# Encoder trunk on one core: four steps of early output products ahead of the conv norm's sums on TensorE in place of two, four between sums and spread, eight behind

## The chip, the cores and the metric

The kernel runs on one core of a Trainium2 chip. A core has TensorE (matrix products), VectorE, ScalarE, GpSimd and SyncE, each with its own in-order list of instructions, which wait for one another through semaphores. TensorE reads its operands from SBUF and writes to PSUM, which has eight banks of 128 x 512 float32 values here. The metric is the device time of one execution in microseconds; the figure for a kernel is the median of its runs.

## The reference

Two layers are computed over a sequence of 512 tokens with 1024 features in float32. Each layer is

```python
x = x + 0.5 * swiglu(rms_norm(x, ffn1_norm[l]), ffn1_w_gate[l], ffn1_w_up[l], ffn1_w_down[l])
h = rms_norm(x, mix_norm[l])
p = h @ w_in[l]
attn = mla_group(...)      # latent attention, 8 heads of 64 value columns, chunk-causal
conv = conv_group(...)     # GLU, causal depthwise convolution (31 taps), layer norm, silu
x = x + jnp.concatenate([attn, conv], axis=-1) @ w_out[l]
x = x + 0.5 * swiglu(rms_norm(x, ffn2_norm[l]), ffn2_w_gate[l], ffn2_w_up[l], ffn2_w_down[l])
x = rms_norm(x, post_norm[l])
```

The part that matters here is the end of the mixing stage. The conv group closes with a layer norm over its 512 columns and a silu:

```python
mu = jnp.mean(xf, axis=-1, keepdims=True)
xc = xf - mu
y = xc * lax.rsqrt(jnp.mean(xc * xc, axis=-1, keepdims=True) + EPS)
return (y * g.astype(jnp.float32) + b.astype(jnp.float32)).astype(x.dtype)
```

Then the output projection takes 1024 columns, the first 512 from the attention heads and the last 512 from the conv group. Its sum over columns can begin with the attention half while the conv half is still being normed.

## The kernel before, in words

Activations lie transposed: 128 features on the partitions, 512 tokens along the row, so a 512-column group is four tiles of 128 x 512. A weight block is one 128 x 1024 tile that holds, for 128 output features, the eight 128 x 128 pieces over the 1024 input features.

Every large product is made of three in a rounded float32 form (`mm3`, L169): both operands are split into a high part and the remainder, and high x high (L170), high weight x low activation (L171) and low weight x high activation (L172) are summed in PSUM. The high part of a weight is a cast on ScalarE (L151). The low part of the first four blocks of the output projection is made by a copy of the negated weight and a DMA that adds (L154, L155), and that of the last four by a subtraction on GpSimd (L157).

The mixing stage of a layer is the function `mix_body`. The heads' work ends with pairs of heads: value products on TensorE (L917, in plain float32, half of the array's columns each), their scaling on VectorE (L920, which reads PSUM), and the split into high and low (L177 on ScalarE, L178 on VectorE). The four pairs give the attention half of the output projection's operand, the list `at`.

The conv group's norm runs beside the last heads, and is a chain over all engines:

- The sum over the four tiles goes through TensorE once (L999) to give the mean on all partitions. VectorE subtracts it from the four tiles (L1001).
- ScalarE squares each tile (L200 for the first, L203 for the other three) and VectorE adds the squares (L207, three additions).
- TensorE sums the squares over the partitions: the *sums* (L214, four small products).
- VectorE scales and adds epsilon (L221), GpSimd takes the power -1/2 (L189), VectorE lays the result on a diagonal (L229), and TensorE copies it to all partitions: the *spread* (L233).
- VectorE multiplies the four tiles by it (L1016), ScalarE applies gain, bias and silu (L1018), and the split follows (L177, L178). This is the conv half, the list `cv`.

The output projection has eight blocks of 128 output features. The first four get their attention half early, as filler between the pieces of that chain. These are the *early steps*: first three steps for each of the four blocks (one for each of the first three pairs of heads, which are complete), then one for each block with the last pair. That makes 16 steps, each of three products (L170 to L172):

```python
steps = [(m, k) for m in range(WOG) for k in range(3)] + [(m, 3) for m in range(WOG)]
...
early_steps(0, EA, heads[H - 1][EARLY])
...
early_steps(EA, EB, sums)
early_steps(EB, len(steps), spreading)
```

Each call carries a lower limit: its products come after the instruction named last (`issue_after`). The first call follows the last head's scores, the second the sums, the third the spread. The norm's chain between the calls is written with high priority. Within these limits a planner sets the order of every engine's list by simulating the program's timeline as it builds it. Then the conv half of blocks 0 to 3 follows, the addition to `x` (L1031), and blocks 4 to 7 in full. In the listings and profiles below the blocks' PSUM tiles are called `ps`, the norm's `cv`, weights' high and low parts `wh` and `wl`.

Of the kernel before, what the change touches and what calls it, by code (L numbers as in the profile page):

```python
# [50 lines left out]
GLUP = 0  # L51
EARLY = "s"
PRELOAD = 1
EA = 2
EB = 6
WOG = 4
CHAIN = 400
WAKE = 10
# [20 lines left out]
def encoder_kernel(ctx: ExitStack, tc: tile.TileContext, xT, consts, vecs, rgain, wgu1, wd1, wdq1,  # L79
# [33 lines left out]
    def tiny(tag, w, dt=FP):  # L113
        return small.tile([P, w], dt, tag=tag, name=nm(tag))
# [28 lines left out]
    def vv(l, name):  # L143
        o, w = VOFF[name]
        return vec[:, l, o:o + w]
# [487 lines left out]
    def mix_body(kpool, l, gx, norm, done):  # L633
# [350 lines left out]
        def early_steps(a, b, behind_):  # L984
            with tc.issue_after(behind_):
                for m, k in steps[a:b]:
                    if k == 0:
                        early.append(bank())
                    group(early[m], wo[m], at, (k,), KD)

        early_steps(0, EA, heads[H - 1][EARLY])
        st = Stats()
# [14 lines left out]
        if PRELOAD:  # L1007
            with behind(heads[H - 1]["exps"]):
                A.activation(tiny("pre", 1), ysum[:, 0:1], AF.Silu)
        early_steps(EA, EB, sums)  # L1010
        early_steps(EB, len(steps), spreading)
        lg, lb = vv(l, "lg"), vv(l, "lb")
# [283 lines left out]
```

## Time and profile before

| | us |
|---|---|
| median of three runs | 1797.07 |
| lowest and highest of them | 1794.69, 1797.32 |
| the profiled execution's own time | 1794.2 |
| its span, first to last instruction | 1792.4 |
| TensorE busy in the span | 1778.5 |
| VectorE, ScalarE, GpSimd busy | 1493.5, 1093.8, 382.1 |

TensorE's granted clock is full for the whole span. A busy TensorE means that products are in flight, not that they run at the peak rate. The stage of interest stands twice in the span, at about 495 to 530 us in the first layer and at about 1383 to 1418 us in the second. In a row of a timeline stand the start, the duration, the engine, the line, the operation, the tiles written and read, the shape, and in brackets the idle time of the engine before it with what ended it.

### The profile page before, as it was taken

Reading aid. Unit: us, or ns where it says so; the run is one execution under the profiler, and the core shown is the slowest. Engines: PE = TensorE matmul, PEld = TensorE weight load, DVE = VectorE, ACT = ScalarE, POOL = GpSimd, SP = SyncE. Lnnn points to the kernel's source line nnn. Section 1 sums busy time; section 2 is a strip of 40 time slices with the busy share of each in tenths; the row PEclk is TensorE's granted clock in tenths of the full one; section 3 lists DMA queues with packets and bytes.
Section 4 is the critical chain, followed back from the end, with each engine's and each line's share of the span. In section 5 each row is a group of like instructions: output and inputs, shape, how many; then the busy total and the mean of one; then the engine's idle time right before and its main releaser. Section 6 shows DMA issues by size and latency. Waiting matters only on the chain.

```text
span 1792.4 us, 29441 instructions
## 1 busy us (share of the span) xinstructions
PE 1778.5 (99%) x11430; PEld 1579.1 (88%) x11430; DVE 1493.5 (83%) x2309; ACT 1093.8 (61%) x1699; POOL 382.1 (21%) x313
## 2 busy tenths in 40 slices
PE   9999999999999999999999999999999999999998
PEld 7899999888678899999888999998976788999997
DVE  7898988689965989898779989876999568989883
ACT  5565756467853575756645757564778435756564
POOL 1000000248722000000310000002585310000002
PEclk9999999999999999999999999999999999999999
DMA  5657575324213466665426575743260126575742
GB/s 170 171 131 182 136 178 123 109 84 127 68 28 96 124 166 162 153 160 131 124 65 171 123 194 122 193 114 111 81 157 21 52 79 170 130 185 131 183 117 74
DMA packets 71947, 228.28 MB, mean 127 GB/s; under 512 B 8448, under 2 KB 9600, under 8 KB 71808
## 3 DMA queue, kind: packets, MB, share of 16 engines
q1 hardware_dynamic: 55536, 171.87, 30.5%
q0 software_dynamic: 16128, 54.53, 18.2%
q8 instruction: 89, 1.46, 0.3%
q14 instruction: 50, 0.41, 0.1%
q10 hardware_dynamic: 144, 0.00, 0.0%
HBM read 222.19 MB, written 2.10 MB: 125 GB/s over the span
## 4 chain that ended last, share of the span: by engine, by line
PE 90%; DVE 6%; ACT 1%; issue 1%; DMA 1%; POOL 0%; SPq 0%; ACTq 0%; DVEq 0%
PE ps L170 24%; PE ps L171 23%; PE ps L172 23%; PE ps L389 11%; PE ps L390 6%; DVE cv L968 1%; DVE mx L876 1%; DMA raw<-in_wgu 1%; PE ps L917 1%; DVE r L898 0%; PE ps L895 0%; PE ps L214 0%; DVE r L855 0%; PE ps L676 0%; DVE wl L262 0%
## 5 line engine op out<-in xcount | busy, mean ns | idle before, releaser
L171 PE MATMUL ps<-r,wh 128*128 128x256 f32 (+1 forms) x2556 | 812.9, 319 | 0.1
L170 PE MATMUL ps<-r,wh 128*128 128x256 f32 (+1 forms) x2556 | 811.0, 320 | 1.1 <-ACT wh L151 0.5
L172 PE MATMUL ps<-r,wl 128*128 128x256 f32 (+1 forms) x2364 | 755.3, 321 | 0.0
L170 PEld LDWEIGHTS ps<-r,wh 128*128 128x128 f32 x2556 | 483.8, 189 | 45.6 <-ACT wh L151 3.7
L171 PEld LDWEIGHTS ps<-r,wh 128*128 128x128 f32 x2556 | 484.6, 190 | 36.4 <-DVE r L178 1.5
L172 PEld LDWEIGHTS ps<-r,wl 128*128 128x128 f32 x2364 | 448.2, 190 | 33.8
L389 PE MATMUL ps<-xj,wh 128*128 128x512 f32 x864 | 303.8, 391 | 0.0
L151 ACT CAST wh<-raw 128x1024 fp32r<-128x1024 f32 (+3 forms) x148 | 132.6, 901 | 216.9 <-PE ps L171 135.3
L260 ACT CAST wh<-fr 128x1024 fp32r<-128x1024 f32 (+1 forms) x160 | 157.8, 986 | 103.8 <-DVE fr L426 49.3
L406 POOL DMA_DIRECT2D ls<-in_wgu x72 | 62.5, 868 | 734.5 <-ACT ls L405 525.0
L157 DVE TENSOR_TENSOR wl<-raw,wh 128x1024 fp32r<-128x1024 f32 (+3 forms) x132 | 141.2, 1077 | 91.0 <-ACT wh L151 90.3
L262 DVE TENSOR_TENSOR wl<-fr,wh 128x1024 fp32r<-128x1024 f32 (+1 forms) x160 | 181.8, 1136 | 20.1 <-ACT wh L260 20.1
L389 PEld LDWEIGHTS ps<-xj,wh 128*128 128x128 f32 x864 | 161.4, 188 | 30.1
L390 PE MATMUL ps<-xj,ls 128*128 128x256 f32 x576 | 161.3, 280 | 0.0
L974 POOL TENSOR_TENSOR y<-y,pr 128x495 f32<-128x495 f32 (+29 forms) x90 | 121.7, 1353 | 46.4 <-ACT pr L972 41.0
L260 ACT CAST wh<-raw 128x1024 fp32r<-128x1024 f32 (+1 forms) x100 | 98.1, 981 | 45.2 <-PE ps L171 24.5
L262 DVE TENSOR_TENSOR wl<-raw,wh 128x1024 fp32r<-128x1024 f32 (+1 forms) x100 | 113.3, 1133 | 14.2 <-ACT wh L260 13.8
L390 PEld LDWEIGHTS ps<-xj,ls 128*128 128x128 f32 x576 | 108.3, 188 | 0.0
L405 ACT ACTIVATE ls<-fr 128x1024 fp32r<-128x1024 f32 (+1 forms) x56 | 56.1, 1002 | 75.9 <-PE ps L390 42.8
L207 POOL TENSOR_TENSOR r<-r,t 128x512 f32<-128x512 f32 x45 | 73.3, 1638 | 136.5 <-ACT t L203 136.2
L968 DVE SCALAR_TENSOR_TENSOR cv<-m,vec,cv 128x511 f32<-128x511 f32 (+14 forms) x120 | 87.8, 732 | 3.8 <-ACT cv L964 2.2
L406 POOL DMA_DIRECT2D ls<-in_wdq x32 | 27.6, 863 | 262.1 <-ACT ls L405 262.1
(257 smaller groups left out, 2919.1 us busy)
## 6 DMA issues: line engine op xcount, KB each, us to landing
fr<-in_wgu SPq DMA_DIRECT2D x112, 512.0 KB, 4.3
ls<-in_wgu POOLq DMA_DIRECT2D x72, 512.0 KB, 6.3
raw<-in_wgu SPq DMA_DIRECT2D x62, 512.0 KB, 4.6
fr<-in_wdq SPq DMA_DIRECT2D x48, 384.0 KB, 5.0
ls<-in_wdq POOLq DMA_DIRECT2D x32, 384.0 KB, 4.8
raw<-in_wd SPq DMA_DIRECT2D x32, 384.0 KB, 3.2
raw<-in_wd SPq DMA_DIRECT2D x32, 256.0 KB, 2.8
raw<-in_wcv SPq DMA_DIRECT2D x16, 512.0 KB, 3.6
```

Of the source, the lines that this page charges most:

```text
L151: order["cast"] = A.copy(hi[:, :w], raw[:, :w]).ins
L157: (G if kind in POOLW.split() else V).tensor_tensor(lo[:, :w], raw[:, :w], hi[:, :w].bitcast(FP), ALU.subtract)
L170: T.matmul(o, lh, rh, start=first, stop=False, skip_group_check=free)
L171: T.matmul(o, lh, rl, start=False, stop=False, skip_group_check=free)
L172: order["mm"] = T.matmul(o, ll, rh, start=False, stop=last, skip_group_check=free).ins
L260: A.copy(hi[:, :w], src[:, :w])
L262: order["lo"] = V.tensor_tensor(lo[:, :w], src[:, :w], hi[:, :w].bitcast(FP), ALU.subtract).ins
L389: T.matmul(o, w[0][:, c], both, start=start and k == 0, stop=False, skip_group_check=True)
L390: last = T.matmul(o[:, 0:HS], w[1][:, c], both[:, 0:HS], start=False, stop=k == 3, skip_group_check=True).ins
L406: G.dma_start(out=lo[:, :n], in_=w, accum_op=ALU.add)
L968: V.scalar_tensor_tensor(acc[:, s:], u[c][:, :S - s], tap(k), acc[:, s:], ALU.mult, ALU.add)
L974: order["conv"] = G.tensor_tensor(ys[c][:, s:], ys[c][:, s:], pr[:, s:], ALU.add).ins
```

## The change

Two constants are different: the first call of early steps makes four steps in place of two, the second still makes four (the fifth to the eighth in place of the third to the sixth), and the third makes the last eight in place of the last ten. No instruction is added or left out.

```diff
-EA = 2
-EB = 6
+EA = 4
+EB = 8
```

The planner makes of it what follows; both layers change in the same way. On TensorE around the sums, `ps_5619` is block 0, `ps_5659` (before) and `ps_5629` (now) is block 1, `ps_5374` the last pair of heads. Ahead of the seven value products that complete this pair, the difference is

```order
 L171 MATMUL ps_5619<-r_5292,wh_5391 128x512
 L172 MATMUL ps_5619<-r_5291,wl_5393 128x512
+L170 MATMUL ps_5629<-m_5156,wh_5398 128x512
 L917 MATMUL ps_5374<-r_5339,m_4774 64x512
 L917 MATMUL ps_5374<-r_5303,m_4783 64x384
```

One product of block 1 went ahead of the seven. Behind them, on the same engine, there stood before

```order
L917 MATMUL ps_5374<-r_5303,m_4801 64x128
L917 MATMUL ps_5374<-r_5346,m_4801 64x128
L214 MATMUL cv_5643<-ones,m_4633 128x1 x4
L170 MATMUL ps_5619<-r_5357,wh_5391 128x512
L171 MATMUL ps_5619<-r_5358,wh_5391 128x512
L172 MATMUL ps_5619<-r_5357,wl_5393 128x512
L170 MATMUL ps_5659<-m_5156,wh_5398 128x512
```

and now there stands

```order
L917 MATMUL ps_5374<-r_5346,m_4801 64x128
L170 MATMUL ps_5619<-r_5357,wh_5391 128x512
L171 MATMUL ps_5619<-r_5358,wh_5391 128x512
L172 MATMUL ps_5619<-r_5357,wl_5393 128x512
L171 MATMUL ps_5629<-m_5157,wh_5398 128x512
L172 MATMUL ps_5629<-m_5156,wl_5400 128x512
L214 MATMUL cv_5650<-ones,m_4633 128x1 x4
L170 MATMUL ps_5629<-r_5291,wh_5398 128x512
```

The sums followed the last value product directly; now five products of blocks 0 and 1 stand between the two.

On VectorE at the same place, where `m_4633` collects the squares and `t_5383` takes the last pair of heads, the difference is

```order
 L207 TENSOR_TENSOR m_4633<-m_4633,m_4058 128x512
 L207 TENSOR_TENSOR m_4633<-m_4633,m_3846 128x512
+L207 TENSOR_TENSOR m_4633<-m_4633,m_4058 128x512
 L920 TENSOR_TENSOR t_5383<-ps_5374,t_5372 128x512
-L207 TENSOR_TENSOR m_4633<-m_4633,m_4058 128x512
 L178 TENSOR_TENSOR r_5386<-t_5383,r_5385 128x512
```

The last addition of squares moved ahead of the scaling of the last pair of heads.

On TensorE around the spread, where `ps_5669` is block 2, there now stands

```order
L172 MATMUL ps_5669<-r_5291,wl_5407 128x512
L233 MATMUL cv_5659<-m_4058,ones 128x512
L170 MATMUL ps_5669<-r_5357,wh_5405 128x512
L171 MATMUL ps_5669<-r_5358,wh_5405 128x512
L172 MATMUL ps_5669<-r_5357,wl_5407 128x512
```

Before, the spread (then `cv_5652`) stood six products earlier, ahead of all products of block 2; it still follows twelve products after the sums. Behind it stand 24 products in place of 30 until the first one that reads the conv half. In the conv half of blocks 0 to 3 the products are interleaved differently, so that block 0 ends six rows later. The lists of SyncE and GpSimd are the same.

## The prediction

> **What bounds the kernel now.** I read the page first, for the engine that fills the span and for the chain that ended last; then the waits of TensorE alone; then the timeline of TensorE, VectorE and ScalarE around the places where it waits.
>
> ```profile
> span 1792.4 us, 29441 instructions
> PE 1778.5 (99%) x11430; PEld 1579.1 (88%) x11430; DVE 1493.5 (83%) x2309; ACT 1093.8 (61%) x1699; POOL 382.1 (21%) x313
> PE 90%; DVE 6%; ACT 1%; issue 1%; DMA 1%; POOL 0%; SPq 0%; ACTq 0%; DVEq 0%
> ```
>
> TensorE is busy for 99% of the span and carries 90% of the last-ended chain. A change pays only if it closes a gap in TensorE's own stream, and a wait of another engine costs nothing until TensorE stands behind it. Its waits, by what ended them, are few:
>
> ```profile
> PE cv L214 <- DVE m L207: 2.8, 2, 1.4
> PE ps L853 <- DVE kn L822: 1.1, 2, 0.9
> PE ps L131 <- DVE ones L127: 1.1, 1, 1.1
> PE ps L872 <- ACT r L880: 0.5, 1, 0.5
> PE ps L170 <- ACT wh L151: 0.5, 2, 0.3
> PE ps L917 <- ACT r L880: 0.4, 2, 0.2
> PE ps L214 <- DVE r L207: 0.2, 1, 0.2
> ```
>
> The first row is the largest and sits exactly where the change works: the sums of the conv group's norm (L214) wait twice, once in each layer, 1.4 us each, for VectorE's last addition of squares (L207). No row names a DMA. The timeline of TensorE in the first layer:
>
> ```profile
> 503.13 0.39 PE L171 MATMUL ps<-m,wh 128*128 128x512 f32 x1
> 503.36 0.40 PE L172 MATMUL ps<-m,wl 128*128 128x512 f32 x1
> ...
> 504.38 2.37 PE L917 MATMUL ps<-r,m 128*64 128x512 f32 x14
> 508.13 1.05 PE L214 MATMUL cv<-ones,m 128*128 128x1 f32 x8 [1.38 <-DVE m L207]
> ...
> 509.82 0.40 PE L170 MATMUL ps<-m,wh 128*128 128x512 f32 x1
> ...
> 510.29 0.39 PE L172 MATMUL ps<-m,wl 128*128 128x512 f32 x1
> ...
> 511.68 0.39 PE L172 MATMUL ps<-r,wl 128*128 128x512 f32 x1
> 511.91 1.02 PE L233 MATMUL cv<-m,ones 128*128 128x512 f32 x2
> ...
> 519.65 1.07 PE L170 MATMUL ps<-r,wh 128*128 128x512 f32 x4
> 520.55 0.39 PE L171 MATMUL ps<-r,wh 128*128 128x512 f32 x1
> ```
>
> In a row the first number is the start, the second the duration; products start 0.23 us apart (503.13 to 503.36), although each is shown as 0.39 long, because they are pipelined. From 506.75 (504.38 + 2.37) to 508.13 TensorE does nothing: 1.38 us. The second layer has the same gap:
>
> ```profile
> 1395.64 1.05 PE L214 MATMUL cv<-ones,m 128*128 128x1 f32 x8 [1.38 <-DVE m L207]
> ```
>
> Why the last addition is late shows on VectorE and ScalarE:
>
> ```profile
> 504.80 0.63 ACT L203 ACTIVATE m<-m 128x512 f32<-128x512 f32 x1 [0.51 <-DVE m L207]
> ```
>
> ```profile
> 504.08 1.48 DVE L207 TENSOR_TENSOR m<-m,m 128x512 f32<-128x512 f32 x2
> 506.79 0.69 DVE L920 TENSOR_TENSOR t<-ps,t 128x512 f32<-128x512 f32 x1 [1.23 <-PE ps L917]
> 507.39 0.68 DVE L207 TENSOR_TENSOR m<-m,m 128x512 f32<-128x512 f32 x1
> 509.22 0.16 DVE L221 TENSOR_SCALAR vtok<-cv 128x4 f32<-128x4 f32 x1 [0.37 <-PE cv L214]
> 510.53 0.69 DVE L229 TENSOR_TENSOR m<-cst,rtok 128x512 f32<-128x512 f32 x1 [1.14 <-POOL rtok L189]
> ```
>
> The last square is there at 505.43 (504.80 + 0.63) and VectorE is free at 505.56, but the addition stands behind L920, which waits for the last value product of the heads (L917). So the sums wait for the heads, which they do not need, and TensorE has nothing in between.
>
> **The change part by part.** Nothing is added or removed; six output products (two steps) of each layer move from behind the spread to ahead of the sums. The order shows one of the six ahead of the seven L917, five between them and the sums, and twelve between sums and spread as before (other twelve). No DMA, POOL or SyncE instruction moves.
>
> Time of the sums. The one early product sends the L917 block 0.23 us later; its end goes from 506.75 to 506.98. Then the five. The first of them follows a float32 product of half width, and what such a switch costs is seen in the chain, where the same L917 to L170 switch stands at 502.86:
>
> ```profile
> 502.86 0.43 PE ps L170
> 503.29 0.23 PE ps L171
> ```
>
> 0.43 in place of 0.23, so 0.20 for the switch. The five take 0.43 + 4 x 0.23 = 1.35 us and end at 506.98 + 1.35 = 508.33. The sums come next: the row pair L172 at 511.68 and L233 at 511.91 shows that a full-width float32 product starts 0.16 before the modelled end of the product ahead (511.68 + 0.39 = 512.07). So L214 starts at 508.17, 0.04 after today's 508.13. Its operand is in time: with the addition now ahead of L920, it runs from 505.56 to about 506.25, 1.9 us before. L920 loses nothing, since it waits for L917 in either order.
>
> [...]
>
> Between sums and spread. Twelve products before, twelve after, so L233 moves by the same 0.04, to 511.95. Its operand (L229) is ready at 511.22 today and at 511.26 then; it stays hidden with 0.7 us to spare.
>
> Behind the spread. Before, 30 products lie between L233 and the first product of the conv half (519.65); after, 24. TensorE arrives there 6 x 0.23 = 1.38 us earlier less 0.04, at 518.31. What it needs there comes from the other engines, which keep their times (plus 0.04):
>
> ```profile
> 515.12 0.60 ACT L177 CAST r<-m 128x512 fp32r<-128x512 f32 x1
> 518.09 0.62 ACT L177 CAST r<-m 128x512 fp32r<-128x512 f32 x1
> ```
>
> ```profile
> 515.76 0.69 DVE L178 TENSOR_TENSOR r<-m,r 128x512 fp32r<-128x512 f32 x1 [0.31 <-ACT r L177]
> 518.90 0.68 DVE L178 TENSOR_TENSOR r<-m,r 128x512 fp32r<-128x512 f32 x1
> ```
>
> The first high half is there at 515.72, the first low half at 516.45, wanted at 518.31 and 519.21: 2.6 and 2.7 us of cover remain of 3.9 and 4.1. The last ones (518.71 and 519.58) are first used 26 and 27 products after 518.31, at about 524.3. This cover hides all of it.
>
> The weights of output blocks 4 to 7. Their buffer comes free with the last product of block 0. The new order puts that product six rows later, so it stays at the same time (six products of 0.23 against 1.34 earlier), and the cast and the subtraction on GpSimd that follow stay too:
>
> ```profile
> 524.83 1.05 ACT L151 CAST wh<-raw 128x1024 fp32r<-128x1024 f32 x1 [6.13 <-PE ps L171]
> ```
>
> ```profile
> 525.96 2.41 POOL L157 TENSOR_TENSOR wl<-raw,wh 128x1024 fp32r<-128x1024 f32 x1 [15.47 <-ACT wh L151]
> ```
>
> ```profile
> 531.46 0.39 PE L172 MATMUL ps<-m,wl 128*128 128x512 f32 x1
> ```
>
> The low part is done at 528.37 and wanted at 531.46 today, at 530.12 then: 1.75 us of cover left of 3.09. After that TensorE goes on without a wait, and the later stages follow its pace; the list of waits above has nothing there that could take the gain back.
>
> The sum: 1.38 - 0.04 = 1.34 us a layer, 2.7 us for two. If the new switch from a product to L214 costs another 0.20, it is 1.14 a layer, 2.3 us; if neither switch costs anything, 2.76 us. I take 2.7, because the rows nearest to the new order give the 0.04. The profiled execution took 1794.2 us with a span of 1792.4, so it would take 1791.5. It lies 2.9 below the median of the three runs shown (1797.07). The four executions known are 1794.2, 1794.69, 1797.07 and 1797.32, two pairs 2.6 us apart, and the median is one of the upper pair. Their mean is 1795.8, and 1795.8 - 2.7 = 1793.1 us is the forecast, 0.22% below the median shown; the mechanism alone is 0.15%.
>
> **The rivals.** First, the change does what it says on TensorE and the gain is given back further on: either the conv half is not ready at 518.31 (it would have to be 2.6 us later than the rows show), or the low weights of block 4 hold TensorE at 530.12 (1.75 us later than shown). For it speaks that both covers shrink by 1.34; against it, that both chains hang on events that keep their time. With everything given back it is 1795.8.
>
> Second, slower: the sums themselves come late. L214 now stands behind six products, and in that queue the high and low halves of the second weight block are wanted at 504.29 and 507.94, 5.5 and 2.4 us sooner than today (509.82 and 510.29). A hold-up there delays sums, spread and the conv half together, while the filler behind the spread is shorter. The first 2.6 us of delay are covered; from 2.6 + 1.34 = 3.9 us a layer on the kernel is slower than before, and with 5.7 us by 2 x 1.8 = 3.6, that is 1799.4. The transfers of the low halves, a layer's four, speak against it:
>
> ```profile
> L155 POOL DMA_DIRECT2D wl<-in_wout x4: 877/896/1180, 437.3 to 452.1; - x4
> DMA to landing us min/median/max: 5.8/8.0/8.8
> ```
>
> The last was issued at 452.1 and had landed by 460.9, 47 us before it is wanted.
>
> Third, the early product of block 1 holds up the heads: it stands ahead of L917 and waits for a PSUM bank that VectorE must have read. Were that read as late as the last addition of squares, at 506.25 instead of 504.29, each layer would lose 1.96 and win 1.34: 0.6 worse, 1797.0 against 1795.8. The bank is the one read by the L920 before, and that row ends at 499.28:
>
> ```profile
> 498.59 0.69 DVE L920 TENSOR_TENSOR t<-ps,t 128x512 f32<-128x512 f32 x1
> ```
>
> **How the numbers follow.** About 0.2%, 3.6 us, is what a measurement of this kernel can tell from no change; the gain of 2.7 us is less than that, so in which pair the new median falls decides whether it counts as faster. The forecast case has 0.82. In it the time is under 1793.5 (0.2% below 1797.07) when the same draw would have given the kernel before under 1796.2; two of the four executions are, by 1.5 and 2.0, and two are over by 0.9 and 1.1, so I give a little over half: 0.48 faster, 0.34 within. Gain given back, 0.08: 0.02 faster, 0.05 within, 0.01 slower. Sums late, 0.05: 0.05 slower. Bank late, 0.05: 0.01 faster, 0.03 within, 0.01 slower. Together 0.51, 0.42 and 0.07. The forecast case alone spans 1794.2 - 2.8 = 1791.4 to 1797.32 - 2.3 = 1795.0. The range goes from 1791.0, a little under its lower end, up to 1796.8, which takes in the case of no gain unless the draw is one of the upper pair.
>
> **What the profile after would show.** Right: no wait of L214 for L207 in TensorE's list; L214 at about 508.2 and L233 at about 511.95 in the first layer; the first conv product at 518.3; VectorE's last L207 at about 505.6, ahead of L920; a span near 1789.7 with TensorE's busy time unchanged. Wrong: a new row of waits at L170 for ScalarE's cast (gain given back), L214 well after 508.3 (sums late), or a pause ahead of the L917 block at 504.3 (bank). A span that falls by 2.7 with a median that does not would say that the draw of the runs, not the mechanism, made the number wrong.

## The result and the profile after

| | kernel before | changed kernel |
|---|---|---|
| median, us | 1796.74 | 1791.80 |
| lowest to highest of nine runs | 1794.69 to 1798.79 | 1791.16 to 1793.62 |
| profiled execution: time | 1794.2 | 1791.6 |
| profiled execution: span | 1792.4 | 1789.8 |

The changed kernel is faster: the ratio of the runs is 0.9976, with a 95% interval of 0.9967 to 0.9986, or 4.3 us out of 1797 (2.5 to 5.9). The two profiled spans lie 2.6 us apart, which the interval just takes in. Whether the runs really differ by more than the profiles, and by what, is the main question of what follows.

The waits of TensorE in the changed kernel:

```profile
PE ps L853 <- DVE kn L822: 1.1, 2, 0.9
PE ps L170 <- ACT wh L1112: 1.1, 1, 1.1
PE ps L131 <- DVE ones L127: 1.1, 1, 1.1
PE ps L170 <- ACT wh L151: 0.6, 2, 0.3
```

The row of the sums (L214 for L207, 2.8 us) is gone. The second row is new and belongs to the first weights of the program, some 490 us ahead of the stage. This execution comes to the stage 0.44 us later than that of the kernel before, by the product that gives the mean (L999, 500.96 in place of 500.52), so 0.44 has to be taken from its times before they are held against the first layer of the kernel before:

```profile
500.52 1.13 PE L999 MATMUL cv<-m,onesm 128*128 128x512 f32 x2
```

The timeline of TensorE in the changed kernel:

```profile
500.96 1.13 PE L999 MATMUL cv<-m,onesm 128*128 128x512 f32 x2
...
504.73 0.40 PE L170 MATMUL ps<-m,wh 128*128 128x512 f32 x1
505.06 2.37 PE L917 MATMUL ps<-r,m 128*64 128x512 f32 x14
507.35 0.50 PE L170 MATMUL ps<-r,wh 128*128 128x512 f32 x1
...
508.38 0.40 PE L172 MATMUL ps<-m,wl 128*128 128x512 f32 x1
508.62 0.95 PE L214 MATMUL cv<-ones,m 128*128 128x1 f32 x8
...
512.30 1.02 PE L233 MATMUL cv<-m,ones 128*128 128x512 f32 x2
...
518.66 1.07 PE L170 MATMUL ps<-r,wh 128*128 128x512 f32 x4
```

Less 0.44, the sums start at 508.18, the spread at 511.86 and the first conv product at 518.22 (519.65 before): 1.43 us saved in this layer. In the second layer the first conv product starts at

```profile
1404.88 1.07 PE L170 MATMUL ps<-r,wh 128*128 128x512 f32 x4
```

and L999 at 1387.19, 17.69 us apart:

```profile
1387.19 1.12 PE L999 MATMUL cv<-m,onesm 128*128 128x512 f32 x2
```

Before they were 19.11 apart:

```profile
1388.03 1.13 PE L999 MATMUL cv<-m,onesm 128*128 128x512 f32 x2
1407.14 1.07 PE L170 MATMUL ps<-r,wh 128*128 128x512 f32 x4
```

That is 1.42 again, 2.85 for both layers. The 0.44 lost ahead of the first leaves 2.41, and the spans end 2.6 apart; the remaining 0.2 lies outside of the two places. VectorE adds the squares without a break:

```profile
504.52 2.28 DVE L207 TENSOR_TENSOR m<-m,m 128x512 f32<-128x512 f32 x3
507.46 0.69 DVE L920 TENSOR_TENSOR t<-ps,t 128x512 f32<-128x512 f32 x1 [0.66 <-PE ps L917]
```

### The profile page after: what moved, and what is told of

Its sections match the earlier page's. It is cut to its first block, busy times and chain, and to the rows that moved or that the text cites. A ratio compares the mean times of both kernels' runs of the same rounds, so it can differ in the third digit from the quotient of the medians.

```text
span 1789.8 us, 29443 instructions
## 1 busy us (share of the span) xinstructions
PE 1777.8 (99%) x11430; PEld 1578.7 (88%) x11430; DVE 1497.1 (84%) x2309; ACT 1093.5 (61%) x1699; POOL 383.9 (21%) x313
## 4 chain that ended last, share of the span: by engine, by line
PE 90%; DVE 6%; ACT 1%; POOL 1%; issue 1%; DMA 0%; SPq 0%; ACTq 0%; DVEq 0%
PE ps L170 24%; PE ps L171 23%; PE ps L172 23%; PE ps L389 11%; PE ps L390 6%; DVE cv L968 1%; DVE mx L876 1%; PE ps L917 1%; POOL sck L189 1%; DVE r L898 0%; PE ps L895 0%; DVE kn L822 0%; DVE r L855 0%; PE ps L676 0%; PE ps L214 0%
## 5 line engine op out<-in xcount | busy, mean ns | idle before, releaser
L170 PE MATMUL ps<-r,wh 128*128 128x256 f32 (+1 forms) x2556 | 811.5, 321 | 2.3 <-ACT wh L1112 1.1
L170 PEld LDWEIGHTS ps<-r,wh 128*128 128x128 f32 x2556 | 483.9, 189 | 47.5 <-ACT wh L151 3.4
L207 POOL TENSOR_TENSOR r<-r,t 128x512 f32<-128x512 f32 x45 | 75.0, 1675 | 132.1 <-ACT t L203 131.6
L496 DVE SCALAR_TENSOR_TENSOR x<-ps,x 128x512 f32<-128x512 f32 x112 | 76.8, 685 | 8.6 <-PE ps L172 8.2
```

What stands on the lines that cost most here:

```text
L170: T.matmul(o, lh, rh, start=first, stop=False, skip_group_check=free)
L496: return V.scalar_tensor_tensor(v, o.rearrange("p (m t) -> p m t", m=2), 0.5 * sign, v, ALU.mult, ALU.add).ins
```

## The experiments

Three theories were set against each other at first. *The pause*: TensorE's idle 1.4 us per layer is closed, and nothing else counts. *The filler* (or *the tail*): products moved ahead of the sums, or fewer behind the spread, pay in themselves. *Something besides*: more is gained than the pause. The runs of the first four kernels share 28 runs of the kernel before on one chip (median 1795.75, 1793.70 to 1798.50), those of the last four 23 runs (median 1796.09, 1794.35 to 1798.69).

### The changed kernel again

> The changed kernel again, for the size. Theory 'the pause' (the change closes a 1.4 us pause of TensorE per layer and nothing else): span about 2.6 to 2.9 us under that of the kernel before, ratio about 0.9985. Rival 'something besides': the medians stay about 4.9 us apart, ratio about 0.9973, and then at least 2 us must be found outside of the two windows around the conv norm.

The edit is the change itself. The median was 1791.59 (1791.11 to 1791.74), the ratio 0.9976 (0.9966 to 0.9986), the profiled span 1790.0. So the medians are 4.2 us apart while the profiles stay near 2.5. This speaks for *something besides*, with about 1.4 us outside of the pause, but the interval of the ratio still just takes in the 0.9985 of *the pause* alone; the spans of the single runs decide it further down.

### VectorE's order alone

```diff
-            V.tensor_tensor(o, po, r, ALU.mult)
+            if h < H - 1:
+                V.tensor_tensor(o, po, r, ALU.mult)
...
+        with tc.issue_after(ordered("added")):
+            o, po, pr = heads[H - 1]["o"]
+            V.tensor_tensor(o, po, pr, ALU.mult)
```

The last pair's scaling is written behind the last addition of squares; TensorE's list is that of the kernel before, product by product. On VectorE the split of that pair (L178) also moves, behind L221.

> Constants as before (2 and 6); only VectorE's last addition of squares is moved ahead of the scaling of the last heads, no output product moves. Theory 'the pause': the sums (L214) start at the end of the last value product, near 506.8 in place of 508.13, the pause is gone, 1.4 us per layer saved, ratio about 0.9985, as the change itself. Rival 'the filler' (only the products moved ahead of the sums pay): the pause is shortened by nothing that TensorE can use, ratio 1.000.

The median was 1791.68 (1791.39 to 1792.53), the ratio 0.9977 (0.9967 to 0.9986): as much as the whole change, without moving one product. The pause is gone from the timeline, where L917 ends at 507.12 (504.75 + 2.37):

```profile
504.75 2.37 PE L917 MATMUL ps<-r,m 128*64 128x512 f32 x14
507.05 1.05 PE L214 MATMUL cv<-ones,m 128*128 128x1 f32 x8
```

From the mean product to the first conv product it is 17.68 us in this layer and 17.67 in the second, 1.45 and 1.44 less than before. *The filler* falls. The sums were held up by an addition that stood behind the wrong instruction, and either cure is enough: bring the addition forward, or give TensorE something to do meanwhile. The ratio again lies below what *the pause* gives, though its interval just reaches there.

### The first number alone

```diff
-EA = 2
+EA = 4
 EB = 6
```

> The first number alone (4 and 6): four steps ahead of the sums, two between sums and spread, ten behind. Theory 'the pause': no wait at L214, but only six products between sums and spread, which end at about 510.4 on the clock of the kernel before, while the spread's operand is ready at 511.2; a new pause of about 0.8 us before L233 per layer, so 0.6 us per layer saved, ratio about 0.9993. Rival 'the filler': the first number alone brings all of it, ratio about 0.9985.

The median was 1793.67 (1792.96 to 1794.95), the ratio 0.9985 (0.9976 to 0.9994). By the ratio alone the rival would have won. The timeline shows the new pause that *the pause* foretold, 0.69 us where 0.8 was worked out:

```profile
511.38 1.10 PE L233 MATMUL cv<-m,ones 128*128 128x512 f32 x2 [0.69 <-DVE m L229]
```

So the saving on the path is near what was expected: from the mean product to the first conv product it is 18.62 us in both layers, 0.5 less than before, where 0.6 was worked out. That is 1.0 us for two, the medians lie 2.1 apart, and 1.1 comes on top; the interval (0.0006 to 0.0024, 1.1 to 4.3 us) can't tell the 2.1 from 1.0 + 1.4. The second number is needed for the full gain: with two steps in place of four between sums and spread, TensorE waits for the spread's operand.

### The second number alone

```diff
 EA = 2
-EB = 6
+EB = 8
```

> The second number alone (2 and 8): the queue ahead of the sums is as before, six steps between sums and spread. Theory 'the pause': L214 still waits 1.4 us per layer, and the spread comes 1.4 us later, inside the 3.9 us of cover that the conv half has: ratio 1.000. Rival 'the tail' (what pays is fewer products behind the spread): ratio under 0.999.

The median was 1796.54 (1794.59 to 1798.65), the ratio 1.0002 (0.9993 to 1.0010): no change, and *the tail* falls. What this run is worth most for is its profile. Its span was 1796.7, over 4 us more than that of the kernel before, with the same pause of 1.38 us. The busy times by stretch (columns: length, PE, PEld, DVE, ACT, POOL busy with their instructions, then the granted clock of TensorE, the busy share of the DMA engines and GB/s) show where most of the 4 us are:

```profile
504.00:506.00 2.00, 2.00 (x14) 1.18 (x13) 1.74 (x3) 1.20 (x3) 0.00 (x0) 1.00 0.00 0
506.00:508.00 2.00, 1.03 (x8) 0.44 (x4) 0.94 (x2) 0.21 (x1) 0.00 (x0) 1.00 0.00 0
508.00:510.00 2.00, 1.59 (x10) 1.50 (x11) 1.20 (x3) 0.41 (x1) 0.26 (x1) 0.84 0.00 0
510.00:512.00 2.00, 2.00 (x7) 1.54 (x5) 0.69 (x1) 0.43 (x1) 0.77 (x1) 0.50 0.00 0
512.00:514.00 2.00, 2.00 (x9) 1.62 (x8) 0.00 (x0) 1.06 (x2) 0.00 (x0) 0.81 0.04 8
514.00:516.00 2.00, 2.00 (x9) 1.31 (x7) 0.00 (x0) 0.00 (x0) 0.00 (x0) 1.00 0.00 0
```

```profile
508.41 1.05 PE L214 MATMUL cv<-ones,m 128*128 128x1 f32 x8 [1.38 <-DVE m L207]
509.32 0.75 PE L170 MATMUL ps<-r,wh 128*128 128x512 f32 x1
509.86 0.63 PE L171 MATMUL ps<-r,wh 128*128 128x512 f32 x1
510.29 0.63 PE L172 MATMUL ps<-r,wl 128*128 128x512 f32 x1
...
512.82 0.40 PE L172 MATMUL ps<-r,wl 128*128 128x512 f32 x1
513.06 0.40 PE L170 MATMUL ps<-r,wh 128*128 128x512 f32 x1
```

Behind the pause the granted clock is 0.50, and products start 0.43 us apart (509.86 to 510.29) in place of 0.23. The loss in these stretches is 2 x (0.16 + 0.50 + 0.19) = 1.70 us, which at the 0.50 of the full stretch is 3.4 us of time. The second layer shows the same:

```profile
1400.00:1402.00 2.00, 2.00 (x7) 1.57 (x6) 0.69 (x1) 0.55 (x1) 0.65 (x1) 0.56 0.00 0
1402.00:1404.00 2.00, 2.00 (x7) 1.57 (x6) 0.00 (x0) 0.94 (x2) 0.00 (x0) 0.59 0.00 0
1404.00:1406.00 2.00, 2.00 (x9) 1.30 (x8) 0.00 (x0) 0.00 (x0) 0.00 (x0) 1.00 0.00 0
```

2 x (0.44 + 0.41) = 1.70 us. Two such drops are 3.4 us of the 4.3 by which the span exceeds that of the kernel before; 0.28 is a later start (L999 at 500.80), and the rest was not followed.

This gave a new theory, *pause and clock*: a pause costs its own length (1.38 us), and in some executions a drop of the clock behind it as well (1.70 us). The 28 runs of the kernel before fall into three bunches by span: 10 between 1791.9 and 1793.1, 13 between 1793.4 and 1794.7, and 5 between 1795.8 and 1796.7. The mean clocks are 0.999 or 1.000 in the first bunch, 0.998 or 0.999 in the second, and 0.997 in the third. A drop of 1.70 us takes 0.001 from the mean clock of a run. A 0.999 alone is no sign of one, because the granted clock also falls behind the last product of the program, where it costs nothing: it is 0.50 from about 1790.9 on in the profile of the kernel before (the last product ends at 1786.3) and from about 1787.3 on in that of the changed kernel (1783.7), and with *VectorE's order alone* the stretch from 1760 to 1790 has a mean of 0.93. Steps of about 1.7 us fit no drop, one, and two; that this is what they are is inferred, since only the profile with two and those with none are at hand. Then, as an estimate from the bunches, 13 + 2 x 5 = 23 of 56 pauses had one, 41%, and a mean execution lost 0.82 x 1.70 = 1.4 us: what was missing. The eight runs of the changed kernel in the same series lie between 1789.3 and 1790.0, in one bunch. The nine runs of the result do not all: three of them lie between 1791.4 and 1791.7, two of these with a mean clock of 0.998, where the other six go from 1789.2 to 1790.7 with 0.999 or 1.000. That is the size of one drop in a kernel whose profile has neither the pause nor a drop there. What lengthened these three stays open; a clock of 0.998 does not come again in the 39 runs of the kernels below and above that leave TensorE no pause there, or 0.2 us at most (8 of the changed kernel, 9 with VectorE's order alone, 11 with the pause filled and 11 with the products alone).

### The pause filled with work that gains nothing

```diff
+        early.append(bank())
+        with tc.high_priority(CHAIN), tc.issue_after(order["value"]):
+            for _ in range(6):
+                warmed = T.matmul(early[1], wo[1][0][:, 0:P], at[0][0], start=True, stop=True).ins
```

Besides, the sums are held behind these six products and the last addition of squares behind the scaling of the heads, as before. Block 1's first real product overwrites what they leave in its bank.

> Constants, step order and VectorE order as before; six products are added in the pause between the last value product and the sums (of a weight and an operand that are at hand, into the bank of block 1, whose first real product overwrites them), so TensorE works through the pause and gains nothing by it. Theory 'pause and clock' (the pause costs 1.4 us per layer, and besides it lets TensorE's granted clock drop to half for 3.4 us in a part of the executions, 1.7 us each): the sums start at about 508.3, no drop in any execution, spans in one bunch at 1792.4 to 1793.0, median about 1.3 us under before, ratio 0.9993. Theory 'pause alone': spans spread over 1792 to 1797 as before, ratio 1.000 or a little over.

The median was 1794.47 (1793.81 to 1795.51), the ratio 0.9993 (0.9984 to 1.0002). The sums start when they always did:

```profile
504.20 2.37 PE L917 MATMUL ps<-r,m 128*64 128x512 f32 x14
506.50 1.66 PE L995 MATMUL ps<-m,wh 128*128 128x512 f32 x6
507.99 1.01 PE L214 MATMUL cv<-ones,m 128*128 128x1 f32 x8
```

3.79 us lie between L917 and L214, 3.75 before (504.38 to 508.13). All eleven spans are between 1792.0 and 1793.7, a little wider than foreseen, with mean clocks of 0.999 or 1.000 (1.000 for the longest), where 18 of the 23 runs of the kernel before beside them were above 1793.7, down to a clock of 0.997. The interval of the ratio just includes 1, but the missing upper bunches are clear: with TensorE at work through the pause, no run shows a drop, and the pause's own cost stays.

### A longer pause

```diff
+                if c == 3:
+                    for _ in range(2):
+                        V.tensor_scalar(st.acc, st.acc, 1.0, None, ALU.mult)
```

> As before, but VectorE multiplies the collected squares by one twice before the sums, so the sums wait about 1 us longer in each layer (a pause of 2.3 to 2.7 us in place of 1.4). The conv half has 3.9 us of cover, so nothing else should be late. Theory 'pause and clock': the drop of the clock comes in nearly every execution and both layers, spans near 1792.5 + 2.2 + 3.5 = 1798, spread narrow again, ratio about 1.0017. Theory 'pause alone': 2.2 us more than before at every point of the same spread, ratio about 1.0012.

The median was 1801.15 (1800.43 to 1802.93), the ratio 1.0032 (1.0020 to 1.0044): more than either theory gave. The waits:

```profile
PE cv L214 <- DVE m L1005: 5.6, 2, 2.8
```

The pause is 2.8 us a layer, longer than meant (2.3 to 2.7) because the split of the last pair (L178) came between the two multiplications, so 2 x 1.4 = 2.8 us come directly. The rest is the clock; the profiled execution had a drop in both layers. The first:

```profile
512.00:514.00 2.00, 2.00 (x6) 1.56 (x6) 0.69 (x1) 0.69 (x1) 0.51 (x1) 0.54 0.00 0
514.00:516.00 2.00, 2.00 (x7) 1.38 (x6) 0.00 (x0) 0.79 (x2) 0.00 (x0) 0.61 0.03 8
```

That is 2 x (0.46 + 0.39) = 1.70 us; the second layer has 0.76 from 1402 to 1404, 0.50 from 1404 to 1406 and 0.94 from 1406 to 1410, 1.72 us. All six runs have a mean clock of 0.998 or less and no span is under 1798.7. The five runs of the kernel before in this series that fit no drop span 1792.6 to 1793.3; with 2.8 + 3.4 the sum is 1798.8 to 1799.5, against 1798.7 to 1799.5 in four runs and 1800.9 and 1801.2 in two; the last two are not accounted for in full.

### The products as filler alone

```diff
-                st.add(ys[c], eng=V, into=(u[2], u[1], diag.rearrange("p a b -> p (a b)"), u[1])[c])
+                with tc.issue_after(heads[H - 1]["scaled"]) if c == 3 else nullcontext():
+                    st.add(ys[c], eng=V, into=(u[2], u[1], diag.rearrange("p a b -> p (a b)"), u[1])[c])
```

The numbers are those of the change; VectorE's order at this place is that of the kernel before.

> The changed kernel (4 and 8) with one swap on VectorE: the last addition of squares behind the scaling of the last heads, as in the kernel before. The products alone fill the pause. Theory 'pause and clock': L214 starts 0.2 us later than in the changed kernel, a pause of 0.2 us per layer is left, no drop of the clock; span 0.4 us over the changed kernel, ratio to before 0.9979. Rival 'VectorE's order' (the earlier addition is what pays): ratio near 1.000.

The median was 1792.60 (1791.84 to 1793.45), the ratio 0.9980 (0.9971 to 0.9989), the spans 1790.1 to 1791.1, none with a clock under 0.999. The sums start 0.40 us behind the last of the five products, 0.24 in the changed kernel:

```profile
508.10 0.40 PE L172 MATMUL ps<-m,wl 128*128 128x512 f32 x1
508.50 1.05 PE L214 MATMUL cv<-ones,m 128*128 128x1 f32 x8
```

So the products alone bring nearly all of it too, and the rival falls. From the mean product to the first conv product it is 17.98 us in both layers, 17.70 and 17.69 in the changed kernel; the planner's swap on VectorE is worth these 0.3 us a layer, 0.6 in all, which the ratios (0.9980 and 0.9976) can't show.

### Twelve and sixteen

```diff
-EA = 2
-EB = 6
+EA = 12
+EB = 16
```

> Twelve steps ahead of the sums, four between sums and spread, none behind. Theory of the cover (the conv half is wanted 2.6 us after it is ready in the changed kernel, and eight steps further ahead cost 8 x 0.69 = 5.5 us of it): TensorE waits about 2.9 us per layer at the first conv product (L170 for ScalarE's cast L177), minus what the planner's other order hides; span about 1789.7 + 5.9 = 1795.6, and with a pause of 2.9 us again drops of the clock, 1.7 us each. Slower than the changed kernel by 0.3 to 0.5%, near the kernel before or slower. Rival (the cover is larger than worked out): no wait, span as the changed kernel's.

The median was 1801.02 (1799.79 to 1801.69), the ratio 1.0028 (1.0017 to 1.0040): slower than the kernel before, and the rival falls.

```profile
PE ps L170 <- ACT r L177: 5.7, 2, 2.8
```

```profile
521.32 1.22 PE L170 MATMUL ps<-r,wh 128*128 128x512 f32 x4 [2.84 <-ACT r L177]
522.35 0.62 PE L171 MATMUL ps<-r,wh 128*128 128x512 f32 x1
522.77 0.63 PE L172 MATMUL ps<-r,wl 128*128 128x512 f32 x1
```

TensorE waits 2.84 us a layer for the conv half, 2.9 were worked out from the cover, and behind the wait products start 0.42 us apart: the clock dropped here as well, at another place, where another engine is waited for.

```profile
522.00:524.00 2.00, 2.00 (x7) 1.57 (x6) 0.77 (x2) 2.00 (x4) 0.00 (x0) 0.59 0.02 4
```

The second layer has a drop too, with 0.83 from 1410 to 1420. The profiled span is 1799.5; 1795.6 as worked out and two drops of 1.7 are 1799.0.

## Why the prediction was right, and which size was off

- *The place and the mechanism were right.* The changed kernel has no wait of L214 for L207. The sums were foreseen at 508.17 and came at 508.18 (less the late start), the spread at 511.95 against 511.86, the first conv product at 518.31 against 518.22. The 0.09 is in the sums, which here take 0.95 us in place of 1.05. The switch from a product to the sums, which the prediction left room for, cost nothing (508.38 to 508.62, 0.24).
- *The switch* from L917 to L170 was priced at 0.43 by the row at 502.86; in the changed kernel the chain has the same:

```profile
507.42 0.43 PE ps L170
507.85 0.23 PE ps L171
```

The 2.76 us of the case in which neither switch costs anything is twice the pause of 1.38 us; no run shows the switch from L917 without its cost, and the 0.43 us stands in its place.

- *What was to be hidden stayed hidden.* No new wait appeared at this place for ScalarE's casts or GpSimd's subtractions, and with twelve steps ahead the stall came out at 2.84 us, as the cover said. The rivals (gain given back, sums late, bank late) left no row in the waits.
- *The profiled span* was foreseen near 1789.7 and is 1789.8.
- *The sum's one term was too small.* The step "1.38 - 0.04 = 1.34 us a layer, 2.7 us for two" priced the pause at its length. That is what executions without a drop show (2.6 by the two profiles, 2.8 by the means of the lowest bunches in one series), but a mean execution of the kernel before also lost about 1.4 us to the clock behind the pause, as estimated from the bunches, and the runs differ by 4.2. Path and clock add up in the other kernels as well: 2.9 + 1.4 = 4.3 with VectorE's order alone (medians 4.1 apart), 1.0 + 1.4 = 2.4 with the first number alone (2.1), and, with the 1.5 of the second series, 2.3 + 1.5 = 3.8 with the products alone (3.5) and 1.5 with the pause filled (1.6). The profile on which the sum was built happened to be an execution without a drop, with a full clock up to the last product; only in the last 1.5 us of its span, behind that product, does it fall, to 0.50.
- *The "two pairs 2.6 us apart"* were taken as the luck of the draw, and the forecast (1793.1) was made from their mean. They were the clue: by their times, 1794.2 and 1794.69 belong with the executions without a drop, and 1797.07 and 1797.32 lie where those with drops lie. Taking the mean brought a part of the missing term in by another door, which is why 1793.1 came nearer to the measured 1791.8 than 1797.07 - 2.7 would have. That part of the number was luck: the mechanism as priced gives 0.15%, the runs differ by 0.24%, and 1791.8 lies close to the lower end of the range (1791.0).

## What to carry to other kernels

A pause of the engine that fills the span may cost more than its length: here the clock fell behind both pauses of 1.38 us in one profile (to 0.50 in a full stretch of the first layer), and 1.70 us more were lost at each. When the runs of a kernel lie in bunches while its profile looks clean, compare the clock of each run before pricing anything. Where a sum waits for an addition on another engine, look first at what stands ahead of that addition in its list: here one instruction in a better place gave as much as moving six products a layer. Filler moved ahead of a chain is free only up to the cover that the chain's end has left: here 2.6 us of it were left, and eight further steps of 0.69 us made TensorE wait 2.84 us.

## What the runs showed of the hardware

- Behind a pause of TensorE of 1.38 us, followed by 0.9 us of one-column products, the granted clock stayed at 1.00 in both layers of the profile of the kernel before, and fell in both layers of that of *the second number alone*: there 1.70 us were lost each time, which at the 0.50 of the full stretch takes about 3.4 us. How often it falls is an estimate from the bunches of the spans: 41% of the pauses in one series (23 of 56), 43% in the other (20 of 46).
- Of the six drops in the three traces that have them, five lost 1.70 to 1.72 us by the granted clock of the stretches. The sixth, in the first layer of *twelve and sixteen*, lost about 1.7 us by the starts of its products, an estimate: from 522.35 to 525.75 eight products start 0.42 to 0.43 us apart in place of 0.23 (1.6 us more), and the four ahead of them take 1.03 us (521.32 to 522.35) in place of 0.91.
- With a pause of 2.8 us all six runs of one kernel had a mean clock of 0.998 or less; of the other (twelve and sixteen) four of six had, and two 0.999. With a pause of 0.69 us none of eleven runs was under 0.999.
- One-column products are not needed for a drop behind a longer pause: in the kernel with twelve and sixteen steps full products follow the pause of 2.84 us directly, and the clock is 0.59 from 522 to 524. Whether they have a part in the drops behind the pause of 1.38 us stays open, as does what decides between a drop and none at the same pause.
